# A list schedule that books the SBUF port shared by VectorE and GpSimd

## The chip, the cores and the metric

The kernel runs on one core of a Trainium2 chip. The metric is device time in microseconds (us) of one launch. Engines are named as the profile names them: PE (TensorE matmul), PEld (its weight loads), DVE (VectorE), ACT (ScalarE), POOL (GpSimd), SP (SyncE, which issues the DMAs). SBUF is the on-chip working memory, PSUM the eight banks that matmuls write to.

## The reference

One decoder layer over 2048 tokens of width 1024, in float32:

```
h = RMSNorm(x); p = h @ W_in                       # 2560 columns
a = pooling mixer(p[pool cols])                     # trailing means of 2/4/8/16 tokens, 64x64 map per group
b = differential attention(p[diff cols])            # 4 heads: (softmax(q1 k1) - lam*softmax(q2 k2)) v, causal
c = stick-breaking attention(p[sb cols])            # 4 heads of 64: sigmoid, running product over keys
x = x + concat(a, b, c) @ W_out
x = x + (silu(h2 @ W_gate) * (h2 @ W_up)) @ W_down  # h2 = RMSNorm(x), width 2816
out = RMSNorm(x)
```

## The kernel before

Every float32 matmul operand is split in a high and a low part, and a product is three matmuls (lines 474 to 476 in most stages). The split is `split`: ACT copies the high part (L415), DVE subtracts it from the source (L416). So each operand of PE passes through ACT and DVE first; the DVE half has two inputs, and they lie in SBUF both, or one of them in PSUM.

The stages: `a1_tile` (norm, transposes and input projection of a tile of 512 tokens, `x W_in`), `attention` for the four tiles (six head pairs each; a pair of differential heads takes maxima L717, exponentials L720, a scaling on POOL L742, a mix of two maps on DVE L763; a pair of stick-breaking heads takes a running product on DVE L806 and a multiplication on POOL L810; both then transpose on PE L672 and multiply by the values), `out_proj` (a norm of the heads' outputs in `norm_rows`, `mixed`: a broadcast on PE L882, its product on DVE L887, a split; then `projected`, L914 to L916), and `mlp`. The MLP is two Strassen-like products (`gate_up` for each half of the tokens, then `down`): sums of weight or activation blocks (`add`, L952) are made on POOL, a few on DVE. `head_out` prepares the second half of the tokens beside the first half's `gate_up`: its `operands` run on POOL, too (L1061), and wait for loads of `h_d`.

No order is written out by hand. Each step is handed to a `Plan` as an operation with an engine, an estimated duration, a priority, what it reads and what it writes. `Plan.schedule` walks through time in the plan's own clock: when an engine comes free it takes, among the operations whose inputs are ready, the one of smallest priority; if that one's buffer isn't free it takes the next. Buffers come from rings over shared SBUF slots and PSUM banks, handed out in the order of their making. What comes out is one list; the kernel is then issued in that order, so each engine and the DMA queue on SP has a fixed order, and an instruction that must wait holds all that stand behind it on its engine. The plan's durations are `act_ns`, `dve_ns`, `mm_ns`, `pool_ns`; two engines can be busy in it at the same time whatever they do.

PE is given other work to fill its waits: matmuls of the next tile's input projection or of the tile before's output projection have late priorities, and are taken where attention has none ready.

Of the kernel before, what the change touches and what calls it, by code (L numbers as in the profile page):

```python
# [95 lines left out]


class Op:
    __slots__ = ("eng", "ns", "fn", "prio", "deps", "need", "bufs", "seq", "ready", "start", "end", "out", "plan")


class Plan:
# [2 lines left out]

    LAG = {"pe": (-110.0, 200.0), "act": (130.0, 140.0), "dve": (130.0, 140.0), "pool": (130.0, 110.0), "dma": (950.0, 950.0)}
    MORE = {"dma": 1080.0, "pe": 0.0}

    def lag(self, e, c):
        return self.LAG[e][e != c] + self.MORE.get(c, 0.0)  # L110

# [3 lines left out]
    def op(self, eng, ns, fn, r=(), w=(), prio=0.0):  # L115
        o = Op()
        o.eng, o.ns, o.fn, o.prio, o.seq, o.out = eng, ns, fn, prio, len(self.ops), []
        deps, bufs = set(), []
        for items, writing in ((r, False), (w, True)):
            for it in items:  # L120
                b, key = it if isinstance(it, tuple) else (it, None)
                keys = list(b.hist) if key is None else [k for k in (key, None) if k in b.hist]
                for k in keys:
                    ws, rs = b.hist[k]
                    deps.update(ws)
                    if writing:
                        deps.update(rs)
                if b.ring is not None and b not in bufs:
                    bufs.append(b)
        for items, writing in ((r, False), (w, True)):  # L130
            for it in items:
                b, key = it if isinstance(it, tuple) else (it, None)
                if writing:
                    if key is None:
                        b.hist.clear()
                    b.hist[key] = ([o], [])
                else:
                    b.hist.setdefault(key, ([], []))[1].append(o)
        o.deps, o.bufs, o.plan = {d for d in deps if d.plan is self}, bufs, self
        for b in bufs:  # L140
            b.users.append(o)
        self.ops.append(o)
        return o

    def schedule(self):
        left = {}
        for o in self.ops:
            o.need = len(o.deps)
            o.ready = 0.0
            for d in o.deps:  # L150
                d.out.append(o)
            for b in o.bufs:
                left[b] = left.get(b, 0) + 1
        future = {e: [] for e in self.ENGINES}

        def rouse(g, at):
            for c in g.waiting:
                heapq.heappush(future[c.eng], (at, c.seq, c))
                heapq.heappush(wake, (max(at, free[c.eng]), c.eng))
            g.waiting = []  # L160

        def retire(g):
            if g.next == g.made:
                while g.free:
                    at, i = heapq.heappop(g.free)
                    for h, j in g.over[i]:
                        h.open[j][0] -= 1
                        h.open[j][1] = max(h.open[j][1], at)
                        if h.open[j][0] == 0:
                            heapq.heappush(h.free, (h.open.pop(j)[1], j))  # L170
                            rouse(h, h.free[0][0])
                            retire(h)

        avail = {e: [] for e in self.ENGINES}
        free = dict.fromkeys(self.ENGINES, 0.0)
        free["dma"] = 1700.0
        for o in self.ops:
            if o.need == 0:
                heapq.heappush(future[o.eng], (0.0, o.seq, o))
        wake = [(free[e], e) for e in self.ENGINES]  # L180
        heapq.heapify(wake)
        done = []
        while wake:
            t, e = heapq.heappop(wake)
            if t < free[e]:
                continue
            fut, av = future[e], avail[e]
            while fut and fut[0][0] <= t:
                _, _, o = heapq.heappop(fut)
                heapq.heappush(av, (o.prio, o.seq, o))  # L190
            o = None
            while av:
                _, _, c = heapq.heappop(av)
                stuck = None
                for b in c.bufs:
                    if b.slot is None:
                        g = b.ring
                        if g.next != b.index or not g.free:
                            stuck = (g, None)
                        elif g.free[0][0] + self.MORE.get(e, 0.0) > t:  # L200
                            stuck = (g, g.free[0][0] + self.MORE.get(e, 0.0))
                        if stuck:
                            break
                if stuck is None:
                    o = c
                    break
                g, when = stuck
                if when is None:
                    g.waiting.append(c)
                else:  # L210
                    heapq.heappush(fut, (when, c.seq, c))
            if o is None:
                if fut:
                    heapq.heappush(wake, (max(fut[0][0], t), e))
                continue
            for b in o.bufs:
                if b.slot is None:
                    g = b.ring
                    b.slot = heapq.heappop(g.free)[1]
                    g.next += 1  # L220
                    rouse(g, t)
                    retire(g)
            o.start, o.end = t, t + o.ns
            free[e] = o.end
            heapq.heappush(wake, (o.end, e))
            done.append(o)
            for b in o.bufs:
                left[b] -= 1
                if left[b] == 0:
                    g = b.ring  # L230
                    end = max(u.end + self.LAG[u.eng][1] for u in b.users)
                    heapq.heappush(g.free, (end, b.slot))
                    rouse(g, end)
                    retire(g)
            for c in o.out:
                c.need -= 1
                c.ready = max(c.ready, o.end + self.lag(e, c.eng))
                if c.need == 0:
                    heapq.heappush(future[c.eng], (c.ready, c.seq, c))
                    heapq.heappush(wake, (max(c.ready, free[c.eng]), c.eng))  # L240
        assert len(done) == len(self.ops)
        done.sort(key=lambda o: (o.start, o.seq))
        return done
# [32 lines left out]
def hybrid_block_kernel(  # L276
# [673 lines left out]
    def add(pl, eng, out, a, b, op, r, w, prio):  # L950
        ns, en = (2.15 * TQ + 144, nc.gpsimd) if eng == "pool" else (dve_ns(TQ), nc.vector)
        pl.op(eng, ns, lambda: en.tensor_tensor(out(), a(), b(), op), r=r, w=w, prio=prio)  # L952

    def mlp(pl, rg, prio0):
# [144 lines left out]
        def gate_up(s, ops, fs, prio, ahead=0.0):  # L1099
# [23 lines left out]
            def sum_(o, a, b, op):  # L1123
                add(pl, "pool", lambda: o.t, lambda: a.t, lambda: b.t, op, [a, b], [o], prio)
# [338 lines left out]
```

## Time and profile before

| | |
|---|---|
| median of 3 runs | 2685.91 us (2684.29 to 2689.05) |
| profiled execution | 2685.21 us, of which the span 2683.3 us (1.9 us lie around it) |
| PE busy | 2582.0 us (96%) |
| PEld busy | 2158.9 us (80%) |
| DVE busy | 1768.1 us (66%) |
| ACT busy | 1323.8 us (49%) |
| POOL busy | 879.9 us (33%) |

Busy time counts an instruction that stands at a port as busy, so a mean duration above that of the same instruction elsewhere is waiting inside it. Matmuls overlap in the record; how fast PE runs is seen in the distance from one start to the next.

### The profile page before, as it was taken

What the parts mean: (1) busy time and instruction counts of PE and PEld (TensorE: products, weight loads), DVE (VectorE), ACT (ScalarE), POOL (GpSimd) and SP (SyncE); (2) the same over time, 40 slices, a digit from 0 to 9 for tenths busy, and PEclk for the clock granted to TensorE, in tenths of its full rate; (3) what the DMA queues carried; (4) which work ended last, traced back from release to release, by engine and by line L of the source; (5) the groups of instructions that cost most, each with busy time, mean ns of one, the idle gap of its engine ahead of it and who ended that gap; (6) DMA issues with size and microseconds to landing.
All of it is one profiled execution on the core that took longest, in us unless ns stands there. A gap on an engine that the chain in (4) does not pass through costs nothing.

```text
span 2683.3 us, 39226 instructions
## 1 busy us (share of the span) xinstructions
PE 2582.0 (96%) x13836; PEld 2158.9 (80%) x13836; DVE 1768.1 (66%) x3127; ACT 1323.8 (49%) x2645; POOL 879.9 (33%) x890
## 2 busy tenths in 40 slices
PE   8989989999999999998899999999999999999998
PEld 6878778878888788878878887887888887888886
DVE  6376977779778888886554554475444447558557
ACT  4265666657767566664433533353333333445444
POOL 2001313222443133241024466544544444132041
PEclk9999999999999999988999999999999999999999
DMA  6776564566455845535632455253222338335333
GB/s 209 243 263 199 198 226 155 169 207 214 137 169 154 274 142 177 197 126 166 198 119 99 168 171 187 107 174 109 103 109 88 113 136 298 104 95 197 93 91 121
DMA packets 192709, 436.41 MB, mean 163 GB/s; under 512 B 21240, under 2 KB 58232, under 8 KB 192512
## 3 DMA queue, kind: packets, MB, share of 16 engines
q1 hardware_dynamic: 192512, 433.91, 48.7%
q8 instruction: 108, 1.77, 0.3%
q14 instruction: 89, 0.73, 0.1%
HBM read 313.77 MB, written 120.06 MB: 162 GB/s over the span
## 4 chain that ended last, share of the span: by engine, by line
PE 62%; DVE 9%; DMA 4%; ACT 3%; issue 2%; POOL 2%; SPq 0%; DVEq 0%; POOLq 0%; ACTq 0%
PE bank L476 15%; PE bank L474 15%; PE bank L475 15%; DVE d L416 3%; PE bank L672 3%; PE bank L648 2%; DVE d L806 2%; PE bank L649 2%; PE bank L915 2%; PE bank L914 2%; PE bank L916 2%; DMA d<-wo_d 1%; POOL d L952 1%; PE bank L817 1%; PE bank L816 1%
## 5 line engine op out<-in xcount | busy, mean ns | idle before, releaser
L474 PE MATMUL bank<-d 128*128 128x512 f32 x2296 | 916.2, 399 | 8.4 <-ACT d L415 4.2
L476 PE MATMUL bank<-d 128*128 128x512 f32 x2296 | 908.6, 396 | 6.7 <-DVE d L416 6.4
L416 DVE TENSOR_TENSOR d<-d 128x512 fp32r<-128x512 f32 (+1 forms) x668 | 608.8, 934 | 458.4 <-ACT d L415 231.7
L475 PE MATMUL bank<-d 128*128 128x512 f32 x2296 | 906.8, 395 | 3.4 <-DVE d L416 3.4
L952 POOL TENSOR_TENSOR d<-d 128x512 f32<-128x512 f32 x336 | 520.6, 1558 | 870.4 <-DVE d L416 610.2
L415 ACT CAST d<-d 128x512 fp32r<-128x512 f32 (+1 forms) x668 | 489.0, 762 | 611.4 <-PE bank L476 364.7
L476 PEld LDWEIGHTS bank<-d 128*128 128x128 f32 x2296 | 433.5, 189 | 111.5 <-DVE d L416 11.0
L474 PEld LDWEIGHTS bank<-d 128*128 128x128 f32 x2296 | 434.7, 189 | 106.6 <-ACT d L415 5.6
L475 PEld LDWEIGHTS bank<-d 128*128 128x128 f32 x2296 | 434.2, 189 | 100.8 <-DVE d L416 5.3
L416 DVE TENSOR_TENSOR d<-bank,d 128x512 fp32r<-128x512 f32 (+4 forms) x381 | 220.0, 604 | 113.6 <-ACT d L415 104.8
L810 POOL TENSOR_TENSOR d<-d 128x512 f32<-128x512 f32 (+3 forms) x160 | 164.4, 1028 | 390.2 <-DVE d L806 323.8
L415 ACT CAST d<-bank 128x512 fp32r<-128x512 f32 (+4 forms) x381 | 187.7, 527 | 184.7 <-PE bank L672 108.2
L720 ACT ACTIVATE d<-bank,d 128x512 f32<-128x512 f32 (+3 forms) x320 | 198.6, 626 | 107.1 <-DVE d L717 102.5
L742 POOL TENSOR_SCALAR d<-d 128x512 f32<-128x512 f32 (+3 forms) x144 | 102.8, 730 | 440.5 <-ACT d L732 394.6
L648 PE MATMUL bank<-d 128*128 128x512 f32 (+3 forms) x480 | 199.9, 417 | 28.8 <-ACT d L720 10.9
L1107 ACT COPY d<-bank 128x512 f32<-128x512 f32 x132 | 77.6, 588 | 257.1 <-PE bank L476 231.9
L717 DVE TENSOR_REDUCE d<-bank 128x1 f32<-128x512 f32 (+3 forms) x320 | 186.8, 602 | 25.1 <-PE bank L649 12.6
L1111 DVE TENSOR_TENSOR d<-bank,d 128x512 f32<-128x512 f32 x176 | 121.1, 688 | 124.6 <-PE bank L476 117.8
L806 DVE TENSOR_TENSOR_SCAN d<-d,bank 128x512 f32<-128x512 f32 (+3 forms) x160 | 174.4, 1091 | 33.3 <-ACT d L798 15.6
L649 PE MATMUL bank<-d 128*128 128x512 f32 (+3 forms) x480 | 176.7, 371 | 0.0
L672 PE MATMUL bank<-ident,d 128*128 128x128 f32 x1088 | 156.3, 276 | 6.5 <-DVE d L763 5.4
L914 PE MATMUL bank<-d 128*128 128x256 f32 x512 | 153.3, 299 | 3.9 <-DMA d<-wo_d 2.8
(134 smaller groups left out, 3563.4 us busy)
## 6 DMA issues: line engine op xcount, KB each, us to landing
d<-in_w_gu_dram SPq DMA_DIRECT2D x88, 512.0 KB, 3.5
d<-in_w_in_dram SPq DMA_DIRECT2D x80, 512.0 KB, 4.9
d<-v_d SPq DMA_DIRECT2D x60, 512.0 KB, 4.3
d<-k_d SPq DMA_DIRECT2D x60, 512.0 KB, 4.8
d<-wo_d SPq DMA_DIRECT2D x52, 512.0 KB, 5.3
d<-q_d SPq DMA_DIRECT2D x48, 512.0 KB, 4.5
g_d<-d SPq DMA_DIRECT2D x66, 256.0 KB, 2.1
d<-g_d SPq DMA_DIRECT2D x66, 256.0 KB, 2.7
```

Source lines behind the costliest of these rows:

```text
L415: pl.op("act", act_ns(n, psum), lambda: nc.scalar.copy(hi(), src()), r=r, w=[whi], prio=prio)
L416: pl.op("dve", dve_ns(n), lambda: nc.vector.tensor_sub(lo(), src(), f32(hi())), r=[*r, *after, whi], w=[wlo], prio=prio)
L474: nc.tensor.matmul(o, a_hi, b_hi, start=first, stop=False, **kw)
L475: nc.tensor.matmul(o, a_hi, b_lo, start=False, stop=False, **kw)
L476: nc.tensor.matmul(o, a_lo, b_hi, start=False, stop=last, **kw)
L648: nc.tensor.matmul(s.t[:, :n], qh.t[:, c0:c0 + P], kt.t[:, r, :n], start=True, stop=False)
L649: nc.tensor.matmul(s.t[:, :n], qh.t[:, c0 + 256:c0 + 256 + P], kt.t[:, r, :n], start=False, stop=j < t)
L672: nc.tensor.transpose(tp.t[:, c:c + P], rows[qb][kb // 4].t[:, (kb % 4) * P:(kb % 4 + 1) * P], ident)
L720: pl.op("act", act_ns(n, True, 2), lambda s=s, n=n, e=e, mc=mc, lc=lc, sm=sm: nc.scalar.activation(e.t[:, :n], s.t[:, :n], AF.Exp, bias=sm ...
L806: pl.op("dve", scan_ns(n), lambda iv=iv, n=n, w=w, s=s, prev=prev: nc.vector.tensor_tensor_scan(iv.t[:, n - 1::-1], w.t[:, n - 1::-1], s.t ...
L914: nc.tensor.matmul(o, m[:, 0, cs], wh.t[:, k % 4, :], start=k == 0, stop=False)
L952: pl.op(eng, ns, lambda: en.tensor_tensor(out(), a(), b(), op), r=r, w=w, prio=prio)
```

## The change

The plan marks operations that use a port: all of POOL, and those of DVE that call a two-input instruction and touch no PSUM buffer. When the plan picks a marked operation at time t while the other engine's last marked operation ends later than t, it puts it back until that end, and takes the next one. Durations, priorities, rings and the program's work are untouched.

```diff
+    PORT = {"dve": "pool", "pool": "dve"}
+    TWO = {"tensor_sub", "tensor_mul", "tensor_add", "tensor_tensor", "scalar_tensor_tensor"}
@@ op
+        psum = any(isinstance(b.ring.slots[0], tuple) for b in bufs)
+        o.port = eng == "pool" or eng == "dve" and not psum and not self.TWO.isdisjoint(fn.__code__.co_names)
@@ schedule
+        port = {e: -1e9 for e in self.PORT}
...
                 _, _, c = heapq.heappop(av)
                 stuck = None
+                if c.port and port[self.PORT[e]] > t:
+                    heapq.heappush(fut, (port[self.PORT[e]], c.seq, c))
+                    continue
...
             o.start, o.end = t, t + o.ns
             free[e] = o.end
+            if o.port:
+                port[e] = o.end
```

Of the plan's 3,122 DVE operations 1,379 are marked, and all 880 of POOL. Counted over the two orders, 1,622 operations of DVE stand at another place of their queue (by 59 places at most), 162 of POOL (by 15), 1,903 of PE's 4,662 (by 88), nearly all of those of PE in attention and in the output projection beside it. In the changed file lines below the diff are 11 higher: L952 is L963, L1061 is L1072, L416 is L427, L887 is L898, L474 to L476 are L485 to L487.

**Place A, POOL, in the MLP's first half,** where `operands` (L1061) stands beside `add` (L952). Before:

```order
L952 TENSOR_TENSOR d<-d 128x512
L1061 TENSOR_TENSOR d<-d 128x256
L952 TENSOR_TENSOR d<-d 128x512
L1061 TENSOR_TENSOR d<-d 128x256 x5
L952 TENSOR_TENSOR d<-d 128x512
L1061 TENSOR_TENSOR d<-d 128x256 x3
L952 TENSOR_TENSOR d<-d 128x512
L1061 TENSOR_TENSOR d<-d 128x256
L952 TENSOR_TENSOR d<-d 128x512
L1061 TENSOR_TENSOR d<-d 128x256
L952 TENSOR_TENSOR d<-d 128x512 x2
```

and in the changed kernel:

```order
L963 TENSOR_TENSOR d<-d 128x512
L1072 TENSOR_TENSOR d<-d 128x256
L963 TENSOR_TENSOR d<-d 128x512
L1072 TENSOR_TENSOR d<-d 128x256 x5
L963 TENSOR_TENSOR d<-d 128x512 x5
L1072 TENSOR_TENSOR d<-d 128x256 x8
L963 TENSOR_TENSOR d<-d 128x512
```

The last five sums of the step were spread over ten rows of L1061; now they stand together, ahead of the next eight.

**Place B, PE, where the second half's `gate_up` begins** (`bank` numbers are PSUM banks, the same product having bank3 before and bank2 now). Before:

```order
L474 MATMUL bank3_222<-d_18577,d_18752 128x512
L475 MATMUL bank3_222<-d_18577,d_18752 128x512
L476 MATMUL bank3_222<-d_18577,d_18765 128x512
L474 MATMUL bank4_226<-d_18554,d_18857 128x512
L475 MATMUL bank4_226<-d_18554,d_18857 128x512
L476 MATMUL bank4_226<-d_18554,d_18866 128x512
```

and in the changed kernel:

```order
L485 MATMUL bank2_218<-d_18582,d_18764 128x512
L486 MATMUL bank2_218<-d_18582,d_18764 128x512
L487 MATMUL bank2_218<-d_18582,d_18784 128x512
L485 MATMUL bank0_210<-d_18598,d_18786 128x512
L486 MATMUL bank0_210<-d_18598,d_18786 128x512
L487 MATMUL bank0_210<-d_18598,d_18800 128x512
```

The product into bank4 came next; now seven groups of three matmuls (four into bank0, three into bank2) stand ahead of it.

**Place C, DVE, at the end of attention,** the products L887 and splits of the last tile's mix for the output projection. Before:

```order
L450 TENSOR_SCALAR d<-d 128x1024 x4
L887 SCALAR_TENSOR_TENSOR d<-d,gvec,bank_210 128x512
L887 SCALAR_TENSOR_TENSOR d<-d,gvec,bank_214 128x512
L416 TENSOR_TENSOR d<-d 128x512 x2
L887 SCALAR_TENSOR_TENSOR d<-d,gvec,bank_210 128x512
L416 TENSOR_TENSOR d<-d 128x512
L919 TENSOR_TENSOR d<-bank_214,d 128x512
```

and in the changed kernel:

```order
L427 TENSOR_TENSOR d<-bank_234,d 128x512
L898 SCALAR_TENSOR_TENSOR d<-d,gvec,bank_210 128x512
L427 TENSOR_TENSOR d<-bank_230,d 128x512
L427 TENSOR_TENSOR d<-d 128x512
L898 SCALAR_TENSOR_TENSOR d<-d,gvec,bank_214 128x512
L427 TENSOR_TENSOR d<-bank_234,d 128x512
L427 TENSOR_TENSOR d<-bank_230,d 128x512
L427 TENSOR_TENSOR d<-d 128x512
L898 SCALAR_TENSOR_TENSOR d<-d,gvec,bank_210 128x512
L427 TENSOR_TENSOR d<-bank_234,d 128x384
```

The last three of the five L887 stood behind attention's end and the MLP's first norms (L450); now they stand some 50 places earlier, between the splits of attention's last transposes (bank_230 and bank_234).

## Rows read from the trace of the kernel before

**Rows 1.** Windows: busy us (xcount) of PE, PEld, DVE, ACT, POOL; clock; DMA; GB/s.

```profile
268.00:1208.00 940.00, 899.00 (x5710) 771.50 (x5709) 775.12 (x1443) 622.47 (x1435) 291.04 (x453) 0.98 0.55 182
1208.00:1360.00 152.00, 133.40 (x1008) 125.71 (x1007) 88.48 (x173) 62.74 (x119) 14.94 (x17) 0.92 0.56 182
1360.00:2240.00 880.00, 871.95 (x3760) 705.49 (x3759) 449.13 (x562) 319.61 (x495) 420.31 (x288) 0.99 0.39 135
2240.00:2290.00 50.00, 44.42 (x184) 33.74 (x183) 41.69 (x46) 17.89 (x32) 23.14 (x14) 1.00 0.76 252
```

**Rows 2.** Groups by shape: busy us, mean ns of one, idle before and releasers.

```profile
L416 DVE TENSOR_TENSOR d<-d 128x512 fp32r<-128x512 f32 x448 | 325.5, 759 | 185.6 <-ACT d L415 183.9 <-DMA x_d<-d 1.3
...
L416 DVE TENSOR_TENSOR d<-bank,d 128x512 fp32r<-128x512 f32 x248 | 164.4, 683 | 90.3 <-ACT d L415 81.8 <-DMA v_d<-d 3.3 <-DMA q_d<-d 3.3
...
L952 POOL TENSOR_TENSOR d<-d 128x512 f32<-128x512 f32 x336 | 520.6, 1558 | 870.4 <-DVE d L416 610.2 <-DMA d<-in_w_gu_dram 78.6 <-ACT d L1005 70.6
```

**Rows 3.** Timeline of POOL and ACT near 1625 us: start, us, instruction, [idle before].

```profile
1622.36 0.74 POOL L1061 TENSOR_TENSOR d<-d 128x256 f32<-128x256 f32 x1 [2.60 <-DMA d<-h_d]
...
1627.39 1.26 POOL L952 TENSOR_TENSOR d<-d 128x512 f32<-128x512 f32 x1
...
1628.68 1.04 ACT L415 CAST d<-d 128x1024 fp32r<-128x1024 f32 x1 [8.61 <-POOL d L952]
```

**Rows 4.** Timeline of PE near 1630 us.

```profile
1630.78 0.80 PE L474 MATMUL bank<-d 128*128 128x512 f32 x1 [3.05 <-ACT d L1107]
1631.37 0.63 PE L475 MATMUL bank<-d 128*128 128x512 f32 x1
...
1636.92 0.41 PE L476 MATMUL bank<-d 128*128 128x512 f32 x1
1637.17 0.39 PE L474 MATMUL bank<-d 128*128 128x512 f32 x1
1637.40 0.39 PE L475 MATMUL bank<-d 128*128 128x512 f32 x1
```

**Rows 5.** Timeline of DVE and POOL, 1800 to 1820 us.

```profile
1805.47 8.55 DVE L416 TENSOR_TENSOR d<-d 128x512 fp32r<-128x512 f32 x5
...
1814.54 1.68 DVE L416 TENSOR_TENSOR d<-d 128x1024 fp32r<-128x1024 f32 x1
...
1802.90 14.46 POOL L952 TENSOR_TENSOR d<-d 128x512 f32<-128x512 f32 x8 [4.29 <-DVE d L416]
```

**Rows 6.** Timeline of PE in the same stretch.

```profile
1812.91 0.50 PE L474 MATMUL bank<-d 128*128 128x512 f32 x1 [1.17 <-ACT d L415]
...
1816.28 0.79 PE L476 MATMUL bank<-d 128*128 128x512 f32 x1 [2.63 <-DVE d L416]
1816.87 0.63 PE L474 MATMUL bank<-d 128*128 128x512 f32 x1
...
1821.14 0.47 PE L475 MATMUL bank<-d 128*128 128x512 f32 x1
```

**Rows 7.** Timeline of PE, 1248 to 1266 us.

```profile
1258.22 0.79 PE L882 MATMUL bank<-d,sel 8*128 8x512 f32 x1 [7.52 <-DVE d L887]
...
1259.37 0.58 PE L914 MATMUL bank<-d 128*128 128x256 f32 x1
...
1264.87 0.30 PE L915 MATMUL bank<-d 128*128 128x256 f32 x1
1265.01 0.28 PE L916 MATMUL bank<-d 128*128 128x256 f32 x1
1265.13 0.28 PE L914 MATMUL bank<-d 128*128 128x256 f32 x1
```

**Rows 8.** Timeline of DVE in the same stretch.

```profile
1257.42 1.42 DVE L887 SCALAR_TENSOR_TENSOR d<-d,gvec,bank 128x512 f32<-128x512 f32 x2 [2.28 <-DMA d<-o_d]
...
1262.30 0.75 DVE L887 SCALAR_TENSOR_TENSOR d<-d,gvec,bank 128x512 f32<-128x512 f32 x1 [2.08 <-DMA d<-o_d]
```

**Rows 9.** Timeline of DVE, where `down` begins.

```profile
2254.09 0.69 DVE L952 TENSOR_TENSOR d<-d 128x512 f32<-128x512 f32 x1 [4.89 <-DMA d<-in_w_down_dram]
```

More of the change, by code (lines that the diff above doesn't have):

```diff
@@ L98 @@
 class Op:
-    __slots__ = ("eng", "ns", "fn", "prio", "deps", "need", "bufs", "seq", "ready", "start", "end", "out", "plan")
+    __slots__ = ("eng", "ns", "fn", "prio", "deps", "need", "bufs", "seq", "ready", "start", "end", "out", "plan", "port")
 class Plan:
```

## The prediction

> **What bounds the kernel now.** I read the busy times by stage first, then the groups by shape on DVE and POOL, then the waits of PE, and last the timelines around each long wait of PE. The table ahead shows PE busy for 96% of the span. By stage [rows 1]: in the MLP's `gate_up` PE idles 8 of 880 us, so there the matmuls are the time. In attention it idles 41 of 940 us with DVE busy for 82% of it, and in the output projection behind attention 18.6 of 152 us at a granted clock of 0.92. So no amount of DVE or POOL time has a price by itself; what counts is which waits of PE go or come.
>
> That DVE and POOL meet at a port is in the groups by shape [rows 2]. The split L416 of 512 columns takes 683 ns where one input lies in PSUM and 759 ns on average where both lie in SBUF; the excess is 448 x 0.076 = 34 us. POOL's sum takes 1558 ns on average. Where both engines have only such work the two alternate: five L416 in 8.55 us, 1.71 us each, beside eight sums in 14.46 us, 1.81 us each [rows 5]. Nearly all of this excess lies beside a busy PE and is worth nothing. Two more things follow a long wait of PE. After 3.05 us of idle the matmuls of 512 columns start 0.43 us apart for a while and then 0.23 us [rows 4], that is half the full clock of 2.4 GHz; a wait costs itself and this tail.
>
> **The change part by part.** The instructions, their number and their sizes stay, so nothing is added to any engine. All that can change is the order, and what the lock costs in that order. I went along PE's longest waits and looked at what now stands ahead of them.
>
> Place A, the MLP's first half. PE waits 3.05 us [rows 4] for an ACT copy; ACT itself stood idle 8.61 us until POOL's sum at 1627.39 us was done [rows 3], with the copy queued behind it. POOL was late since its queue held an `operands` step that waited 2.60 us for a load of `h_d` [rows 3], and five rows of that kind among the sums. In the changed order the five sums stand together ahead of the next eight `operands`, so ACT's cast is released before it is due, and the wait goes. What `operands` makes is not needed until shortly before B, over 100 us later, so pushing it back by up to seven places (0.74 us each where nothing blocks it [rows 3]) costs nothing. Gain: the wait 3.05, and the slow tail: 13 steps from 1631.37 to 1636.92 us take 5.55 us, against 13 x 0.23 = 3.0, so 2.5 [rows 4]. Bounds 0 (another wait stands right behind) and 5.6. I take 5, near the upper end, since PE's whole idle time in `gate_up` is 8 us [rows 1], and A and B are 6.8 of it: little else is waiting to come up.
>
> Place B, the second half's start. PE waits 1.17 us and 2.63 us for ACT's and DVE's halves of a 1024 wide split [rows 6], which DVE reaches at 1814.54 us, after the five L416 that alternated with POOL [rows 5]. Changed: 21 matmuls stand ahead of this product. At 0.23 us they cover 4.8 us, more than the 3.8 us. Their inputs were split by DVE long before, in the order on DVE, and they fill another bank. Gain: 3.8, and the tail from 1816.87 to 1821.14 us, 10 steps in 4.27 us against 2.3, so 2.0 [rows 6]. On DVE a product from PSUM now goes ahead of that split, which makes it later by some 0.6 us. Bounds 0 and 5.8; I take 4, because the next step's weights come at the same pace and PE arrives at them earlier.
>
> What the lock allows is shown at B itself: five splits of about 0.68 us and their neighbours on POOL cannot run together, whatever the order, as long as both queues hold nothing else. The Trainium skill (SBUF — State Buffer, Who interferes with whom) says that a DVE instruction with two SBUF inputs and a GpSimd instruction that reads SBUF exclude each other, the second one to issue being blocked until the first is done. The 1.71 us fit it. By that rule B's splits don't come sooner and the gain is the cover alone, the 4 above; without it they would take 5 x 0.68 = 3.4 us and the 5.8 would be whole, the sum below 19 and not 17.
>
> Place C, the end of attention. PE waits 7.52 us for L887 on DVE [rows 7], and DVE in turn 2.28 and again 2.08 us for loads of `o_d` [rows 8]. Those loads go through two slots, each free again only after the split, so five of them make a chain. The change puts the whole chain some 50 DVE places earlier, among the last splits of attention, since PE's filler matmuls ahead of it are used up earlier. The chain keeps its loads, and now the splits behind each L887 wait as well; PE has only six filler groups there. So I count one wait of about 2 us per round, two rounds [rows 8], as staying, some 4 of the 7.5. The slow tail is 25 steps from 1259.37 to 1264.87 us in 5.5 us against 25 x 0.12 = 3.0, so 2.5 [rows 7]; shorter waits keep half of it. Gain: bounds 10 (7.5 and the tail, all gone) and -6 (all five loads wait 2.2 us ahead of the splits, 11 us, with two tails of 2.5, for the 10 before). I take 5.
>
> Place D, the start of `down`. PE idles 5.6 of 50 us [rows 1]. DVE stood 4.89 us for a load of `w_down` [rows 9]; in the changed order that load stands 20 places earlier on SP, and four sums of POOL for a later product move behind the ones that are due, each of which can hold DVE for 1.71 - 0.68 = 1 us [rows 2, 5]. Bounds 0 and 5; I take 2, since the loads come through one queue which itself waits for DVE.
>
> Attention, places 268 to 1208 us. Here the order of PE moves by up to 88 places, mostly fillers that come sooner, as the plan now thinks DVE slower. The work is the same, PE idles 41 us in all [rows 1], and I see no wait that must go or come. I take 0, with bounds of 10 either way, a quarter of those 41. At the end the last splits stand 8 to 12 places ahead of the row norms; 1 us at most, beside the finishing rows, so I take 1.
>
> Sum: 5 + 4 + 5 + 2 + 1 = 17. The profiled execution took 2685.2 us, 0.7 below the median, so 2668 by it and 2669 by the median. I forecast 2669.
>
> **The rivals.**
> - Nothing in effect. The plan's clock drifts from the chip's over 2.7 ms, so what it keeps apart meets anyway, and a place or two of difference doesn't reach PE. For it: POOL's order is nearly the same, 162 of 880 moved. Against: A and B don't rest on the drift, since there it is the queue order that holds the work. Time: about 2684.
> - Slower, by booked waits that aren't there. The plan counts every POOL operation as holding the port, the tiny copies and memsets of the stick-breaking heads too, and puts scans and PSUM splits ahead of mixes (L763) and weight splits which on the chip could have run. In attention both feed PE, and DVE has little room at 82% [rows 1]. If PE's idle there grows by two thirds, 41 to 68 us, while A to D give 14, the time is 2685 + 27 - 14 = 2698. It decides from 41 + 17 = 58 us on. Against: PE's fillers cover most waits there, and now come sooner.
> - A larger gain. Attention gains as well: a quarter of 41, 10 us, and A, B and D reach their upper ends (0.6, 1.8 and 3 more): 15 more in all, 2654. For it: the same fillers that move at C move in all of attention. Against: no long wait there is named that must go.
>
> **How the numbers follow.** The forecast gets 0.62, no effect 0.15, slower 0.13, larger gain 0.10. A difference under 0.2% (5.4 us) can't be told from none here. Of the forecast's 0.62 I leave 0.03 inside this bound; slower gets 0.13 and a fifth of the no-effect case (0.03); so faster 0.59 + 0.10 = 0.69, same 0.03 + 0.12 = 0.15, slower 0.16. The range reaches to the larger gain below, 2654, and to 2692 above, which leaves out the upper half of the slower case.
>
> **What would show it.** A: no wait of PE over 1 us between 1600 and 1640 us, and ACT's 8.61 us idle cut; POOL's five sums in one run. B: PE goes through, with granted clock 1.00 where it fell to half. C: the 7.5 us wait is split in smaller ones ahead of attention's end. D: DVE doesn't stand for `w_down`. Wrong would be: as many us of new PE waits in attention as A to D give, or, for A, a new wait of the same length some 20 us on, which would mean that POOL's total work, not its order, was late.

## The result, and the profile after

The changed kernel takes 2645.68 us in the median of four runs (2643.82 to 2647.66), the one before 2687.16 us on the same chip (2684.29 to 2689.05): ratio 0.9847, 95% interval 0.983 to 0.9864. It is faster by 41 us; the forecast was 2669, and 2645.7 lies below the range. The profiled execution took 2644.44 us, its span 2642.6.

The windows of the changed kernel, by the stages of [rows 1] and with their columns. The stretches are cut where PE has done the same amount of matmul columns as at the cuts of the kernel before:

```profile
272.90:1193.80 920.90, 888.50 (x5713) 772.03 (x5712) 756.45 (x1432) 608.81 (x1411) 284.40 (x434) 0.98 0.56 186
1193.80:1337.80 144.00, 135.84 (x1005) 126.94 (x1004) 98.29 (x185) 74.90 (x144) 24.04 (x35) 0.94 0.55 184
1337.80:2205.70 867.90, 866.04 (x3760) 702.05 (x3759) 447.37 (x560) 319.53 (x494) 417.69 (x289) 1.00 0.40 137
2205.70:2250.80 45.10, 43.22 (x184) 33.95 (x183) 39.17 (x47) 17.67 (x32) 21.04 (x14) 1.00 0.80 276
```

Each stage is shorter: attention by 19.1 us, the output projection by 8.0, `gate_up` by 12.1, the start of `down` by 4.9. These make 44.1; the stretch ahead of them takes 4.9 us more (272.9 against 268). (The experiments below end attention earlier, at 1112.2 us of the kernel before, and count its last part with the output projection; so the 19.1 here are 14.2 there.) PE's idle time in attention went from 41 to 32.4 us, in `gate_up` from 8.0 to 1.9.

The groups by shape, DVE and POOL, against [rows 2]:

```profile
L427 DVE TENSOR_TENSOR d<-d 128x512 fp32r<-128x512 f32 x448 | 322.6, 752 | 172.3 <-ACT d L426 168.8 <-DMA x_d<-d 2.8
...
L427 DVE TENSOR_TENSOR d<-bank,d 128x512 fp32r<-128x512 f32 x248 | 163.7, 683 | 97.6 <-ACT d L426 97.2
...
L963 POOL TENSOR_TENSOR d<-d 128x512 f32<-128x512 f32 x336 | 518.1, 1550 | 829.7 <-DVE d L427 588.5 <-DMA d<-in_w_gu_dram 86.2 <-ACT d L1016 46.8
```

By these mean durations the two engines lose nearly as much at their port as before: 752 ns for 759, 1550 for 1558. What the plan books was hardly avoided on the chip. What is left as a source of the gain is the order.

**Place A.** Timelines of POOL and ACT (start, us, instruction, [idle before]) at the sums of [rows 3]:

```profile
1593.72 6.33 POOL L963 TENSOR_TENSOR d<-d 128x512 f32<-128x512 f32 x4 [1.16 <-DVE d L427]
1600.01 6.95 POOL L1072 TENSOR_TENSOR d<-d 128x256 f32<-128x256 f32 x8
```

```profile
1599.82 0.63 ACT L1125 ACTIVATE d<-d 128x512 f32<-128x512 f32 x1 [2.93 <-DVE d L1122]
1600.36 1.03 ACT L426 CAST d<-d 128x1024 fp32r<-128x1024 f32 x1
```

The sums stand together ahead of eight `operands`, and ACT's wide cast has no idle time ahead of it where it had 8.61 us. PE doesn't wait there.

**Place B.** Timelines of PE, DVE and POOL at the second half's start, against [rows 5, 6]:

```profile
1787.10 0.50 PE L485 MATMUL bank<-d 128*128 128x512 f32 x1 [1.35 <-ACT d L1118]
```

```profile
1775.50 9.21 DVE L427 TENSOR_TENSOR d<-d 128x1024 fp32r<-128x1024 f32 x7
```

```profile
1777.45 10.89 POOL L963 TENSOR_TENSOR d<-d 128x512 f32<-128x512 f32 x7 [3.55 <-DMA g_d<-d]
```

The product that waited 1.17 and 2.63 us now doesn't wait. The one wait left, 1.35 us, stands ahead of another product, one of the seven groups put in front, and is for ACT's copy L1118, not for the split (L427). No slow tail follows: that row's matmul takes 0.50 us, not 0.79, and the granted clock from 1760 to 1803 us is 1.00 (0.93 from 1789 to 1836 us before). DVE and POOL still alternate: 9.21 us for seven splits (six of 512 columns, one of 1024), 10.89 us for seven sums, 1.56 us each, against 1.30 for a sum with DVE idle (below, D).

**Place C.** PE's waits (total us, times, longest) from 1193.8 to 1337.8 us, where the kernel before had [rows 7]:

```profile
PE bank L925 <- DMA d<-wo_d: 2.7, 2, 1.4
PE bank L485 <- ACT d L426: 2.4, 1, 2.4
PE bank L926 <- DMA d<-wo_d: 1.7, 2, 0.9
PE bank L893 <- DVE d L930: 1.2, 1, 1.2
```

The 7.52 us are gone; none of the waits left is for L898 (L887 before), and over the whole span DVE waits only 1.6 us for `o_d` ahead of it.

**Place D.** Timelines of DVE, POOL and PE where `down` begins, against [rows 9]:

```profile
2220.95 0.69 DVE L963 TENSOR_TENSOR d<-d 128x512 f32<-128x512 f32 x1 [5.54 <-DMA d<-in_w_down_dram]
```

```profile
2217.83 1.29 POOL L963 TENSOR_TENSOR d<-d 128x512 f32<-128x512 f32 x1 [9.35 <-DMA d<-in_w_down_dram]
2219.74 1.30 POOL L963 TENSOR_TENSOR d<-d 128x512 f32<-128x512 f32 x1 [0.63 <-DMA d<-in_w_down_dram]
```

```profile
2238.00 0.50 PE L487 MATMUL bank<-d 128*128 128x512 f32 x1 [1.18 <-DVE d L427]
```

DVE stands for `w_down` as long as before (5.54 for 4.89 us). But two of POOL's sums are done before DVE's load lands, and PE idles 1.9 us here (its longest wait is the row shown) and not 5.6.

**The start** lost time that the forecast had not. PE and DVE of the changed kernel:

```profile
61.00 0.76 PE L485 MATMUL bank<-d,bdh 128*128 128x512 f32 x1 [3.80 <-DVE d L427]
...
63.40 0.80 PE L485 MATMUL bank<-d,bdh 128*128 128x512 f32 x1 [0.78 <-ACT d L541]
```

```profile
56.93 1.23 DVE L427 TENSOR_TENSOR d<-d 128x1024 fp32r<-128x1024 f32 x1 [1.38 <-ACT d L426]
58.36 1.83 DVE L427 TENSOR_TENSOR d<-d 128x1024 fp32r<-128x1024 f32 x2 [0.21 <-ACT d L426]
60.10 0.75 DVE L427 TENSOR_TENSOR d<-bank,d 128x256 fp32r<-128x256 f32 x2
```

DVE of the kernel before in the same stretch:

```profile
56.03 0.69 DVE L416 TENSOR_TENSOR d<-d 128x512 fp32r<-128x512 f32 x1 [0.69 <-ACT d L415]
56.64 0.75 DVE L416 TENSOR_TENSOR d<-bank,d 128x256 fp32r<-128x256 f32 x2
57.52 2.36 DVE L416 TENSOR_TENSOR d<-d 128x1024 fp32r<-128x1024 f32 x2
```

Two small splits from PSUM, which PE's next product needs, stood ahead of the wide weight splits at 56.64; now they stand behind them at 60.10 (ACT's halves of these five splits changed places in the same way). PE waits at once, and matmuls of 0.76 and 0.80 us follow.

### The profile page after: what moved, and what is told of

Read it like the earlier page. It is cut to its first block, busy times and chain, and to the rows that moved or that the text cites. A ratio compares the mean times of both kernels' runs of the same rounds, so it can differ in the third digit from the quotient of the medians.

```text
span 2642.6 us, 39218 instructions
## 1 busy us (share of the span) xinstructions
PE 2568.7 (97%) x13836; PEld 2159.9 (82%) x13836; DVE 1753.0 (66%) x3127; ACT 1322.1 (50%) x2645; POOL 876.9 (33%) x890
## 4 chain that ended last, share of the span: by engine, by line
PE 70%; DVE 5%; DMA 4%; ACT 2%; issue 1%; SPq 0%; POOL 0%; DVEq 0%; ACTq 0%; POOLq 0%
PE bank L487 17%; PE bank L485 17%; PE bank L486 17%; PE bank L683 3%; PE bank L659 2%; DVE d L427 2%; PE bank L660 2%; PE bank L926 2%; PE bank L925 2%; PE bank L927 2%; DMA d<-wo_d 1%; PE bank L828 1%; PE bank L827 1%; PE bank L783 1%; PE bank L784 1%
## 5 line engine op out<-in xcount | busy, mean ns | idle before, releaser
L485 PE MATMUL bank<-d 128*128 128x512 f32 x2296 | 914.0, 398 | 4.0 <-ACT d L426 2.4
L487 PE MATMUL bank<-d 128*128 128x512 f32 x2296 | 906.4, 395 | 2.0 <-DVE d L427 2.0
L427 DVE TENSOR_TENSOR d<-d 128x512 fp32r<-128x512 f32 (+1 forms) x668 | 604.8, 928 | 443.7 <-ACT d L426 219.3
L963 POOL TENSOR_TENSOR d<-d 128x512 f32<-128x512 f32 x336 | 518.1, 1550 | 829.7 <-DVE d L427 588.5
L487 PEld LDWEIGHTS bank<-d 128*128 128x128 f32 x2296 | 432.0, 188 | 104.4 <-DVE d L427 4.2
L485 PEld LDWEIGHTS bank<-d 128*128 128x128 f32 x2296 | 433.4, 189 | 99.9 <-ACT d L426 2.6
L427 DVE TENSOR_TENSOR d<-bank,d 128x512 fp32r<-128x512 f32 (+3 forms) x381 | 219.3, 605 | 122.5 <-ACT d L426 122.0
L426 ACT CAST d<-bank 128x512 fp32r<-128x512 f32 (+3 forms) x381 | 186.9, 528 | 171.6 <-PE bank L683 110.4
L659 PE MATMUL bank<-d 128*128 128x512 f32 (+3 forms) x480 | 199.0, 415 | 19.4 <-ACT d L731 8.4
L1118 ACT COPY d<-bank 128x512 f32<-128x512 f32 x132 | 77.5, 588 | 247.1 <-PE bank L487 225.2
L683 PE MATMUL bank<-ident,d 128*128 128x128 f32 x1088 | 155.7, 278 | 1.8 <-DVE d L774 1.7
```

Of the source, the lines that this page charges most:

```text
L426: pl.op("act", act_ns(n, psum), lambda: nc.scalar.copy(hi(), src()), r=r, w=[whi], prio=prio)
L427: pl.op("dve", dve_ns(n), lambda: nc.vector.tensor_sub(lo(), src(), f32(hi())), r=[*r, *after, whi], w=[wlo], prio=prio)
L485: nc.tensor.matmul(o, a_hi, b_hi, start=first, stop=False, **kw)
L487: nc.tensor.matmul(o, a_lo, b_hi, start=False, stop=last, **kw)
L659: nc.tensor.matmul(s.t[:, :n], qh.t[:, c0:c0 + P], kt.t[:, r, :n], start=True, stop=False)
L683: nc.tensor.transpose(tp.t[:, c:c + P], rows[qb][kb // 4].t[:, (kb % 4) * P:(kb % 4 + 1) * P], ident)
```

## The experiments

Three theories of the part in attention. T1: the right operations yield at the right times. T2: any new order of this size moves attention by 10 us or more, and this one was a good draw. T3: it is enough that the plan takes DVE and POOL for slower. "Attention" below is the stretch between equal amounts of PE's work, 194.8 to 1112.2 us in the kernel before, "its end" the one to 1377.1 (end of attention and output projection), "the MLP" the rest.

**e1 and e2: the change in the MLP alone, and ahead of it alone.**

```diff
+        o.port = o.port and prio > 5.9e6     # e1
+        o.port = o.port and prio < 5.9e6     # e2
```

> Marks kept in the MLP alone; attention and the output projection are ordered as before. If the gains add up by place, as the distance between the two traces says (6.4 us at A, 5.5 at B, 4.9 at D, 1.7 at the end), this gains 16 to 19 us on the kernel before: about 2669. If the order in attention is what sets the later places free, it gains less than 8 us.

> Marks kept in all that stands ahead of the MLP, none in the MLP. If the gains add up: the start loses 5, attention gains 15, C 8 and the output projection 4, so 22 us faster than before, about 2665, with the waits at A and B of the kernel before still there. If the lock matters in the MLP only, no difference from before.

e1: 2668.59 us (2663.98 to 2669.29), ratio 0.9939 (0.9917 to 0.9961). e2: 2666.06 us (2665.84 to 2666.36), 0.9933 (0.9912 to 0.9954). Against 2685.3 that is -16.7 and -19.2, together -35.9 of 41; the stages add but for some 5 us. e1 alone gives the forecast's 2669 with no part of attention and none of C, so that match is chance. At equal work e1 gains 6.2 at A, 5.8 at B, 3.4 at D; e2 keeps the loss at the start and gains nothing at A or B.

**e3 and e4: other operations booked.** e3 marks the 749 two-input operations of DVE that touch PSUM, e4 a hashed 1,386 of all.

```diff
-        ... eng == "dve" and not psum and not self.TWO.isdisjoint(...)
+        ... eng == "dve" and psum and not self.TWO.isdisjoint(...)              # e3
+        ... eng == "dve" and (o.seq * 2654435761 >> 7) % 1000 < 442            # e4
```

> The wrong operations are marked: two-input DVE operations that do touch PSUM (749 of them) in place of those that don't. Theory 1, the gain comes from knowing which operations exclude each other: no gain, 2680 to 2700. Theory 2, any other order may come out as far off as this one: anywhere from 2640 to 2720. Theory 3, the plan only has to see POOL and DVE as slower than it did: half the gain or more, 2645 to 2668.

> As many DVE operations marked (1,386 of 3,122) but drawn by a hash of their number. Theory 1: no gain, 2680 or more, and slower than before if false holds cost as the slower rival said. Theory 2: anywhere. Theory 3: half the gain or more, 2645 to 2668.

e3: 2688.82 us, ratio 1.0016 (1.0005 to 1.0028). e4: 2678.99 us, 0.9976 (0.9963 to 0.9989). At equal work both gain the 6 us of A all the same: the sums stand closer together in their orders too, and in that of e5 below, which books nothing (why, in the plan, was not followed up). Attention loses 13.7 us in e3 and 1.2 in e4. A is not due to the right marks; attention's gain seemed to be.

**e5: no booking, but the measured delay added to the plan's durations.**

```diff
+        if eng == "pool":
+            names = fn.__code__.co_names
+            o.ns += 270 if "tensor_tensor" in names else 70 if "tensor_mul" in names else 90 if ... else 0
+        elif o.port and ns > 400:
+            o.ns += 80
+        o.port = False
```

> Nothing is booked. In its place the plan's durations get the mean of what operations were measured to lose: +270 ns for POOL's two-input sums, +70 and +90 ns for its other products, +80 ns for the marked DVE operations over 400 ns. If it is enough that the plan sees POOL and DVE slower, so that PE's fillers come sooner, attention gains its 15 to 20 us and the time is 2645 to 2668. If the marks have to be at the operations that really meet, attention gains nothing: A's sums are clustered in part (2 to 6 us), at B one group stands ahead as before (0), D's load stands as in the changed kernel (3 to 5), so 2675 to 2680. If any new order is a draw, attention may come out anywhere from +15 to -15 us.

2670.99 us (2668.34 to 2672.37), ratio 0.9947 (0.993 to 0.9964). Neither of the first two expectations holds: attention gains 9.4 us (908.0 for 917.4), its end loses 1.3, the MLP gains 6.5 with A in it. The third, a draw, allows it. T3 may give part of the gain, but one such order doesn't tell it from a draw.

**e7 and e8: only one engine yields.**

```diff
-                if c.port and port[self.PORT[e]] > t:
+                if e == "dve" and c.port and port[self.PORT[e]] > t:      # e7; "pool" in e8
```

> The marks stay, but only DVE is put back while POOL holds the port; POOL begins whenever it is ready. If attention's gain comes from what DVE takes first (the heads' pieces that touch PSUM ahead of weight splits), it stays: attention and output projection -20 us; A's five sums are spread as before (0), B keeps one group ahead (0), D's load is early (-3 to -5): 2660 to 2665. If it comes from POOL stepping back, attention gains nothing and the time is about 2680.

> The mirror image: only POOL is put back while DVE holds the port. A's sums are clustered (-6), B has five groups ahead (-5), D's load is late (0). If attention's gain comes from what DVE takes first, attention gains nothing: 2672 to 2676. If it comes from POOL stepping back, -20 more: 2652 to 2656.

e7: 2661.64 us (2651.62 to 2662.66), 0.9905 (0.9881 to 0.9929). e8: 2672.41 us (2668.59 to 2679.68), 0.9952 (0.9937 to 0.9967). Attention and its end gain 21.1 us in e7 and 2.1 in e8: there it is DVE's order that counts. (The traced execution of e7 took 2651.62 us, 10 less than its other three, that of e8 7 more than its median; part of this difference can come from that.) A gains 6.1 in e8, as expected. B gains less than 3 of the expected 5: with five groups ahead of the late product PE still waits 1.15 and 0.63 us. In e7, A gains 4.0 and B 3.0 where nothing was expected.

**e9 to e12: which operations, and when.** All four touch only attention and the output projection without the first tile, and only DVE yields.

```diff
+        o.port = o.port and -1e6 + 0.6 < prio < 5.9e6
-                if c.port and port[self.PORT[e]] > t:
+                if e == "dve" and c.port and t < t // 3000 * 3000 + 1000:      # e9: a made-up holder
...
+        o.port = eng == "pool" or eng == "dve" and (o.seq * 2654435761 >> 7) % 1000 < 224   # e10; >> 11 in e11
...
-                heapq.heappush(av, (o.prio, o.seq, o))
+                heapq.heappush(av, (o.prio + 1e7 * (e == "dve" and o.port), o.seq, o))      # e12: no port
```

> Only DVE is put back, only in attention and the output projection (381 operations, the first tile not), and not by what POOL does: a made-up holder has the port during the first 1.0 us of every 3.0 us of the plan's clock, about POOL's share of the time. POOL is never put back. A, B and D stay as before. If attention gains because DVE takes its work on PSUM ahead of splits and mixes now and then, whenever that is, this gains it as well: 16 to 22 us, 2664 to 2670. If the putting back has to fall on POOL's real operations, it gains nothing: 2683 to 2690.

> The other half of that question: DVE is put back while POOL holds the port in the plan, in the same stretch, but the operations that yield are 388 drawn by a hash of their number, on PSUM or not. If it matters which operations yield, attention gains little: 2680 to 2688, with 5 us or so from the end of attention at most, where the order of L887 moves as in the changed kernel. If any reordering of this size gains, 2664 to 2670.

> A second draw of 390 operations, the same otherwise, for the spread between draws: the same two expectations, 2680 to 2688 or 2664 to 2670. If the two draws lie more than 10 us apart, a single schedule of this kind says little about its rule.

> The 381 right operations always go behind any ready unmarked operation of DVE, whatever POOL does; no port at all. If the gain is simply that splits and mixes yield to the work on PSUM, this gains as much or more: 2658 to 2668. If yielding all the time starves PE of split operands, it loses part: 2670 to 2695.

e9: 2687.63 us (2683.18 to 2695.46), 1.0004 (0.9991 to 1.0016). e10: 2658.55 us (2652.57 to 2662.33), 0.9893 (0.987 to 0.9917). e11: 2666.61 us (2664.92 to 2668.54), 0.9926 (0.9907 to 0.9944). e12: 2701.17 us (2698.0 to 2704.94), 1.0055 (1.0034 to 1.0075). e12 is slower than both its expectations. The right operations at wrong times gain nothing, and random ones at the right times gain 27.6 (e10) and 19.5 us (e11), no less than e2. As a rule for the whole gain, the first half of T1, that the right ones must yield, falls. In attention alone the random ones gain 7.0 and 5 us, half of the 14.2 at most; the rest of theirs is in its end. The windows of e9, then of e10 (attention, its end):

```profile
196.80:1121.60 924.80, 885.29 (x5587) 764.65 (x5586) 742.39 (x1413) 602.78 (x1397) 269.67 (x421) 0.97 0.56 186
1121.60:1384.90 263.30, 240.65 (x1685) 217.37 (x1683) 179.79 (x322) 132.59 (x259) 50.69 (x75) 0.93 0.50 161
```

```profile
192.40:1102.80 910.40, 876.15 (x5598) 758.57 (x5597) 733.43 (x1390) 594.90 (x1374) 260.28 (x417) 0.99 0.58 190
1102.80:1352.30 249.50, 233.78 (x1676) 211.08 (x1675) 189.47 (x348) 140.84 (x283) 51.51 (x79) 0.98 0.50 164
```

**e14 and e15: the two kinds of work that yield.** The yielding operations of DVE are the heads' mixes (e14) or the projections' splits (e15).

```diff
+        o.port = o.port and -1e6 + 0.6 < prio < 5.9e6 and (eng == "pool" or 0 <= prio)   # e14; prio < 0 in e15
```

> DVE is put back while POOL holds the port in the plan, POOL never is, only in attention and the output projection, and of DVE only the work of the heads yields: 160 mixes (L763 before) and 48 of the small operations beside them. If attention's gain comes from the mixes, which can wait while PSUM is drained, the 13 us up to the end of attention's last tile come whole, with some 5 to 9 behind it since L887 moves part of the way: 2664 to 2668. If it comes from the top-priority splits, 0 to 5 us: 2681 to 2686.

> The other 173 of the same stretch: the splits and norms of the input and output projections, which otherwise stand ahead of everything on DVE. L887 stays where it was (nothing at the end of attention). If attention's gain comes from these no longer being first, 8 to 13 us: 2673 to 2678. If it comes from the mixes, 0 to 3 us: 2683 to 2686.

e14: 2671.36 us (2669.65 to 2674.85), 0.9949 (0.9934 to 0.9963). e15: 2699.38 us (2697.39 to 2705.11), 1.0049 (1.0032 to 1.0066), slower than before. Windows of e14, then of e15:

```profile
194.50:1105.90 911.40, 879.27 (x5596) 761.97 (x5595) 734.30 (x1403) 601.83 (x1390) 259.49 (x417) 0.98 0.57 189
1105.90:1363.70 257.80, 238.41 (x1677) 216.14 (x1676) 180.48 (x334) 134.99 (x266) 51.41 (x79) 0.95 0.50 164
```

```profile
194.80:1132.80 938.00, 896.36 (x5594) 768.26 (x5594) 746.49 (x1419) 607.25 (x1406) 266.83 (x421) 0.97 0.55 183
1132.80:1394.80 262.00, 236.59 (x1679) 215.49 (x1678) 175.16 (x317) 129.25 (x250) 48.96 (x75) 0.94 0.50 163
```

None of the expectations of e14 and e15 holds. In attention the mixes alone give -6.0 us, the projections alone +20.6, both together (e7) -12.3. What an order gives there is no sum over its parts, and yielding at POOL's times in the plan doesn't suffice: e15 does that, with right operations, and is the slowest of all in attention. T1 falls, and T3 covers a part at most. T2 is left in a weaker form: the order counts, but of the twelve new orders of attention only four (the changed kernel, e3, e7, e15) move it by 10 us or more.

**e16 and e17: both kernels, unchanged, for a second trace.**

> The kernel before, unchanged, for a second trace: how far two traces of one order lie apart in each stage. 2684 to 2690 us; the stretches (first 195 us, attention, its end with the output projection, the MLP) within 3 us of the first trace, if differences of 5 us and more between orders are to be believed.

> The changed kernel, unchanged, for a second trace: 2643 to 2648 us, the stretches within 3 us of its first trace, the wait at 61 us there again.

2682.09 and 2645.14 us. Windows of the kernel before and then of e16:

```profile
194.80:1112.20 917.40, 881.69 (x5592) 759.16 (x5591) 739.40 (x1405) 601.59 (x1391) 267.74 (x419) 0.98 0.57 187
1112.20:1377.10 264.90, 240.76 (x1681) 216.00 (x1680) 183.06 (x332) 134.09 (x265) 51.35 (x78) 0.93 0.49 159
```

```profile
193.10:1110.50 917.40, 880.11 (x5592) 757.93 (x5591) 739.21 (x1405) 602.13 (x1391) 267.93 (x419) 0.99 0.57 187
1110.50:1371.70 261.20, 238.73 (x1681) 214.51 (x1681) 181.87 (x332) 134.03 (x265) 52.59 (x78) 0.94 0.49 162
```

Of the changed kernel, its first trace and then e17:

```profile
199.10:1102.30 903.20, 874.38 (x5595) 759.81 (x5594) 723.87 (x1381) 592.68 (x1368) 267.81 (x415) 0.98 0.58 191
1102.30:1354.40 252.10, 239.55 (x1679) 217.15 (x1678) 189.35 (x356) 141.40 (x289) 53.72 (x82) 0.95 0.49 164
```

```profile
198.60:1101.90 903.30, 874.18 (x5594) 759.64 (x5593) 723.47 (x1381) 592.85 (x1368) 267.99 (x415) 0.98 0.58 191
1101.90:1354.50 252.60, 240.03 (x1679) 216.80 (x1678) 189.29 (x356) 141.46 (x289) 53.80 (x82) 0.95 0.49 164
```

Attention repeats within 0.1 us in each pair, but the end of the order before only within 3.7, more than the 3 expected. More traces repeat these orders. In attention e2, e6, e18 and e19 have the changed kernel's order, and e1 has that of the kernel before; in its end too, but for 27 places of DVE in e1 and e2. Both stretches in e19:

```profile
201.70:1103.20 901.50, 871.61 (x5594) 756.92 (x5593) 723.03 (x1381) 592.86 (x1368) 268.00 (x415) 0.99 0.58 192
1103.20:1356.70 253.50, 239.91 (x1679) 216.61 (x1678) 189.43 (x356) 141.66 (x289) 53.53 (x82) 0.95 0.49 163
```

Six traces of the changed order give 901.5 to 905.1 us in attention and 249.9 to 254.9 in its end, three of the order before 917.4 to 918.2 and 261.2 to 267.4. The ranges don't meet, so the 14.2 us in attention belong to the order, and so does a gain in its end. An order with one trace is less sure where that execution's whole time lies off the others: in e7 it is 10 us below them, in e8, e9 and e15 6 to 7 above the median.

**e6, e18 and e19: the change without the first tile's marks.** e18 is e6 once more, e19 the changed kernel on the same chip as e18.

```diff
+        o.port = o.port and prio > -1e6 + 0.6
```

> The changed kernel, but nothing of the first tile's work (the start) is marked, so that its five DVE splits at 57 us keep their place. If the +5 us at the start comes from those, they go and the rest stays: 2645.7 - 5 = 2641, ratio to the kernel before 0.983. If the order at the start isn't the cause, 2645 to 2646 again.

> The kernel of e6 beside the changed one on one chip. In e6's trace (2645 us) the 5 us of the start are gone but attention and its end take 4.7 us more than in the changed kernel; its other three runs took 2634 to 2636. If the start's 5 us are a real gain, 2636 to 2641 here, and 5 to 9 below the changed kernel; if attention gives them back, 2644 to 2646, level with it.

> The changed kernel, unchanged, timed on the same chip: 2643 to 2648 us by either theory.

e6: 2636.02 us (2633.83 to 2645.17), ratio to before 0.9825 (0.9801 to 0.9848). e18: 2638.50 us (2637.57 to 2641.33), 0.9828 (0.9813 to 0.9843). e19: 2645.71 us (2643.89 to 2649.03), 0.9854 (0.9839 to 0.987). The runs of e18 and e19 don't overlap: leaving the first tile unmarked gains 7.2 us on the changed kernel, and this version is the fastest measured, 47 us below the kernel before. DVE of e18 at the start:

```profile
55.91 0.69 DVE L428 TENSOR_TENSOR d<-d 128x512 fp32r<-128x512 f32 x1 [0.69 <-ACT d L427]
56.52 0.75 DVE L428 TENSOR_TENSOR d<-bank,d 128x256 fp32r<-128x256 f32 x2
57.40 2.36 DVE L428 TENSOR_TENSOR d<-d 128x1024 fp32r<-128x1024 f32 x2
```

The two small splits stand ahead again, and PE's longest wait between 50 and 66 us is 0.8 us, as in the kernel before. What moves them is POOL being put back: e8, where it alone is, has the five splits in the changed order and PE's wait,

```profile
59.97 0.77 PE L485 MATMUL bank<-d,bdh 128*128 128x512 f32 x1 [3.80 <-DVE d L427]
```

and e7, where DVE alone is put back, has neither.

## Why the prediction was right and wrong

The direction was right, and so were the places in the MLP and at attention's end. Sizes were too small everywhere, and in attention the step itself failed. Measured parts, as time at equal work against the first trace of the kernel before:

| part | forecast | measured | what showed it |
|---|---|---|---|
| start | none | +4.9 (e17: +4.2) | e18: gone with the first tile's marks; e8: there with POOL alone put back |
| attention | 0, bounds 10 either way | -14.2 | e1, e2, e6, e16 to e19: repeats; e3 to e15: depends on the order |
| C and output projection | -5 | -12.8 | e16, e18: one order's traces lie 4 to 5 apart |
| A | -5 | -6.1 | e1, e3 to e6, e8, e17 to e19: sums closer together, no wait of PE; e2, e9 to e12, e14, e15: POOL's order as before, PE waits 2.98 to 4.67 us |
| B | -4 | -5.1 | e1: with eight groups ahead (the seven and the one before); e2: without |
| D | -2 | -4.9 (e17 to e19: -3.8 to -4.0) | e1, e7: with the early load; e2, e8: without; e4 doesn't fit |
| end | -1 | -1.7 | not tried apart |

They add up to -39.9 of the -40.9 at the last point compared; the stretches between the places hold the rest.

**The step that failed** is "I see no wait that must go or come. I take 0" for attention, which gained 14.2 us, and with it the bound of a quarter of PE's idle time. One long wait did go: PE's 4.66 us for `k_d` at 401 us, longer than the 3.05 of place A, is 1.69 us in the changed kernel. The rest is spread over short ones. PE's waits in attention before (total us, times, longest), 268 to 1208 us:

```profile
PE bank L648 <- DMA d<-k_d: 6.4, 2, 4.7
PE bank L648 <- DVE d L806: 6.3, 6, 2.3
PE bank L648 <- ACT d L720: 5.8, 9, 1.7
PE bank L672 <- DVE d L763: 5.4, 6, 1.6
```

and after, 272.9 to 1193.8 us (L659 is L648, L683 is L672):

```profile
PE bank L659 <- DVE d L817: 5.6, 8, 1.6
PE bank L659 <- ACT d L731: 3.6, 6, 1.0
PE bank L659 <- DMA d<-k_d: 3.1, 2, 1.7
...
PE bank L683 <- DVE d L774: 1.7, 2, 1.3
```

`k_d` gives 3.3 us and the mixes 3.7, ACT's exponentials 2.2. The bounds of 10 were a quarter of the idle time; but the stretch shrank by 14.2 us where PE's idle time fell by 7 (917.40 - 881.69 against 903.20 - 874.38 us), and 8 in the second pair of traces. The other half lies in PE's busy time, 881.69 against 874.38 us for the same work. Little of that is slow tail as in [rows 4]: the granted clock of the stretch is 0.98 before and after, 0.99 and 0.98 in the second pair. But a matmul's row lasts 0.39 us where the next starts after 0.23 [rows 4], so a delay of up to 0.16 us counts as busy time. Matmuls at full clock with no listed wait behind them whose next start comes over 0.1 us later than their columns need at 2.4 GHz lose 56.6 us in all before and 51.1 after, 57.5 and 51.3 in the second pair. A bound from idle time alone left these short delays out.

Why this order is among the good ones stays open. e2 and e6 have the changed kernel's order in attention, so DVE yields at POOL's times in eight different orders: five are 5 to 14 us shorter in attention (the changed one, e7, e10, e11, e14), e4 is level, e3 and e15 are 14 and 21 longer. No theory of the three covers all of them.

A number that could have been read ahead of any run is the plan's own clock. Each kernel's `Plan.schedule` can be run by itself. At equal columns of PE's matmuls it gives, for the changed order against the one before, 3.6 us more at the start, 0.9 less in attention and 8.5 less in its end with the output projection. So the plan itself had the loss at the start and most of the gain at C; what it didn't have is attention.

**C.** "One wait of about 2 us per round" staying was too careful: no wait of PE over 1 us for L898 stayed. The chain stands at DVE's places 1830 to 1846 of its queue (1871 to 1893 before), so its loads land while attention's last splits run. End of attention and output projection took 249.5 to 254.9 us in the orders with the chain's first product at 1817 to 1830 (e2, e6, e10, e11, the changed kernel), 256 to 266 at 1842 to 1852 (e5, e7, e8, e14), 261 to 270 at 1871 to 1885 (both traces of before, e3, e9, e12, e15). e4 with 1812 but 262.5 doesn't fit, so the place isn't all of it; in the plan's own clock, too, this stretch of e4 is 2.4 us longer than before, where the orders of the first group are 8.5 to 9.7 shorter. The rest of the 12.8 is the output projection, for which no term stood.

**A and B** came as told, near or above their upper ends, with the granted clock at 1.00 in `gate_up` (0.99 in [rows 1]). The nearly full sum of wait and tail was the right term; taking off 0.6 and 1.8 for what stands behind was not borne out. B's cover must be large: five groups ahead (e8) left 1.8 us of waits at the late product, eight left none in any of six traces; the product that still waits (0.46 to 1.35 us) is another. The Trainium skill (SBUF — State Buffer, Who interferes with whom) has a DVE instruction with two SBUF inputs and a GpSimd instruction that reads SBUF block each other; B's 1.56 us per sum after the change, against 1.30 beside an idle DVE, agree. So B's splits still meet the sums, and the gain at B is put down to cover, as forecast; no run took the cover away and left the rest.

**D.** "DVE doesn't stand for `w_down`" was wrong, it stands 5.54 us. The gain is there with POOL's two sums going ahead of DVE's load. By e1 and e7 (-3.4, -5.4, load at SP's place 1060) against e2 and e8 (+2.7, +1.2, places 1080 and 1078) it goes with the load's place; but e4, with the load at 1061, lost 3.2 us there, and the order before repeats only within 1.4 (e16), so this is likely and not shown.

**The start** was not looked at; PE's order is the same there. DVE's was not: five splits had changed places, and PE waited for one of them. The sum held no term for it.

**The rivals.** "Nothing in effect" and "slower" did not come; but the doubt behind the first was right, what the plan keeps apart meets anyway. "A larger gain" (2654) had attention as the place of more, by 10 us, and was 8 us short; most of that is C's, for which it kept the 5. That fillers made the gain in attention, as it says, is not shown.

## What to carry to other kernels

Where a scheduler makes the order, a new rule in it is a new draw of all the orders behind it: compare with placebo rules of the same reach before the rule gets the credit. Price each long wait of PE with its slow tail, and give a stage whose order moves by many places wide bounds instead of nothing because no single wait must go: here PE's busy time moved as much as its idle time. Run the plan for both kernels and compare its own clock stage by stage before forecasting. Look at every stage where any engine's order moved, the start too: five splits that changed places cost 5 us, and taking the rule away there gave the fastest version.

## What had not been expected of the hardware

- The time lost at the port barely fell (752 for 759 ns, 1550 for 1558), and still the kernel gained 1.5%.
- One order repeats closely on the chip in attention: 917.4 to 918.2 us in three traces of one, 901.5 to 905.1 in six of another, beside a spread of some 35 us between orders of the same work.
- Waits of 2.18 and 0.94 us at B in e7 left the granted clock of that stretch (1765 to 1809 us) at 1.00; 2.29 and 2.40 us in e2 went with 0.93 (1766 to 1814 us).
